# A two-layer encoder trunk in split float32: the second SwiGLU's first column pair as Strassen products, the root mean square from a table, and smaller moves

## The chip, the cores and the metric

The kernel runs on one core of one Trainium2 chip. The metric is the device time in microseconds, as the median of the runs. A profiled execution is a run of its own, with a time of its own.

## What is computed

Two layers over 512 tokens of width 1024, each a half-step SwiGLU, a mixer (gated convolution and latent attention with a rotation of the positions), a second half-step SwiGLU and a gated projection of a per-layer input; then a last norm. The functions that the change touches:

```python
def rmsnorm(x, g):
    xf = x.astype(jnp.float32)
    y = xf * lax.rsqrt(jnp.mean(xf * xf, axis=-1, keepdims=True) + EPS)
    return (y * g.astype(jnp.float32)).astype(x.dtype)

def swiglu(x, w_gu, w_down):
    g, u = jnp.split(x @ w_gu, 2, axis=-1)
    return (jax.nn.silu(g) * u) @ w_down

def apply_rope(x, cos, sin):
    ...
    return jnp.concatenate([x1 * cos - x2 * sin, x2 * cos + x1 * sin], axis=-1).astype(x.dtype)

def reference(...):
    h = x
    for i in range(DEPTH):
        h = h + 0.5 * swiglu(rmsnorm(h, ffn1_norm[i]), ffn1_w_gu[i], ffn1_w_down[i])
        u = rmsnorm(h, mix_norm[i])
        ...
        h = h + merged @ w_o[i]
        h = h + 0.5 * swiglu(rmsnorm(h, ffn2_norm[i]), ffn2_w_gu[i], ffn2_w_down[i])
        gate = jax.nn.sigmoid(rmsnorm(h, ple_norm[i]) @ w_ple_gate[i])
        h = h + gate * (p[i] @ w_ple_proj[i])
    return rmsnorm(h, final_norm)
```

## The kernel before

**Split numbers.** All matrix work is float32 by three products: each operand is split into a rounded part (ACT's cast, names that end in h) and the rest (DVE's subtraction, names that end in l), and PE multiplies hh, lh and hl (`mm3`, L209 to L211). Weights stream from HBM in packed blocks of 128x1024: SP loads one into `st`, ACT makes `wh` (L67), DVE makes `wl` (L68). Four such pairs are in use at a time, and ten raw blocks.

**Strassen products.** Most wide products are done in 2x2 blocks with seven products instead of eight. `Quad.part` gives the weight sums (L138 to L149, each a DVE step of 128x1024, ahead of another wh and wl), `Halved.row` the token sums of row j (L379 to L386: x and y scaled on ACT, four DVE steps of 128x256 into t and u, then the splits th, tl, uh, ul). `Sevens.step(n, j)` issues product j of column pair n into three PSUM banks (tiles b0nb, b0nc, b0na); products 1, 5 and 6 are copied out by ACT (L434). Product 1 uses the split x of rows 0 to 3, product 5 the left half of t, 6 and 4 the halves of u, 7 the right half of t, 2 and 3 the split x of rows 4 to 7.

**One SwiGLU (`ffn`).** Its name is a0 or a1 (first SwiGLU of layer 0 or 1), b0 or b1 (second). `normed` splits the eight blocks of h as they become final and sums their squares; `rms` turns the sum into r = 1/rms, by which the products are scaled afterwards. The first columns are computed whole, without Strassen, over the eight blocks x0 to x7 (4 gate and up pairs in a0, 2 elsewhere); PE has this work while DVE forms the token sums. In a1 rows 0 and 1 of the token sums stand ahead, among the last blocks of h; in b0 and b1 all four come after h. Then come the Strassen products, each pair's last ones alternating with the next pair's first, and the down projection.

**What sets the order.** There is no planner: each engine runs its instructions in one queue, in the order that results from the program's order and the scheduler's priorities. A step that waits holds up all behind it on its engine.

**rms.** A matmul with ones sums the squares over the partitions (ps); DVE scales (L282), ACT takes the root (L283, after a table load), DVE takes the reciprocal (L284) and a Newton step (L285 to L287).

**The end.** The last block's sigmoid, product and sum (L870 to L873), squares on ACT (L887), a PE sum (`fss`), DVE, ACT and DVE for 1/rms (L919 to L926), then the scaled output tiles `fo` (L932, L934) and their DMAs.

## Time and profile before

| | us |
|---|---|
| median of 3 runs | 2299.07 (2299.01 to 2299.6) |
| profiled execution, its own time | 2300.29 |
| its span | 2298.4 |
| PE busy | 2278.3 (99%) |
| DVE busy | 1866.4 (81%) |
| ACT busy | 1123.8 (49%) |
| mean granted clock of PE | 0.997 |

The span runs from the first instruction to the last write; the profiled execution's own time is 1.89 us longer. PE's busy share counts pipelined matmuls, so it doesn't show small holes; waits do. Time lies in the timeline by its start from the span's start: a0 begins at 0, b0's first matmul is at 747.42, a1 begins near 1148, the last output is issued at 2294.18.

### The profile page before, as it was taken

To read this page: it belongs to the slowest core of one execution; us is meant where nothing else is said; L and a number is where in the kernel's file an instruction comes from. 1 tells how busy PE (TensorE), PEld (TensorE's weight loads), DVE (VectorE), ACT (ScalarE), POOL (GpSimd) and SP (SyncE) were. 2 spreads that over 40 slices of the span, in tenths; PEclk is the share of its full clock that TensorE was granted. 3 is DMA by queue.
4 is the path that set the end of the run, shared out by engine and by line. 5 is a ranking of instruction groups with operands and counts; after the bars stand their busy time and mean duration, and the time that the engine had idled before them with its cause. 6 is when DMAs were issued, how large, how long until landed. Compare 5 with 4: busy or idle time off the path is not lost.

```text
span 2298.4 us, 34687 instructions
## 1 busy us (share of the span) xinstructions
PE 2278.3 (99%) x14168; PEld 2061.6 (90%) x14168; DVE 1866.4 (81%) x2577; ACT 1123.8 (49%) x1682; POOL 36.8 (2%) x42
## 2 busy tenths in 40 slices
...
GB/s 193 110 92 103 100 142 92 55 120 120 55 61 87 65 120 101 102 111 129 82 74 111 102 101 115 118 89 74 108 104 56 74 73 101 103 100 101 110 83 38
DMA packets 63087, 222.76 MB, mean 97 GB/s; under 512 B 7248, under 2 KB 7248, under 8 KB 62928
## 3 DMA queue, kind: packets, MB, share of 16 engines
...
q10 hardware_dynamic: 720, 0.84, 0.1%
q14 instruction: 48, 0.39, 0.1%
...
## 4 chain that ended last, share of the span: by engine, by line
PE 93%; DVE 5%; ACT 1%; issue 1%; DMA 0%; ACTq 0%
PE a0pd L209 2%; PE a1pd L209 2%; PE b0pd L209 2%; PE b1pd L209 2%; PE b1pd L210 2%; PE b0pd L210 2%; PE a1pd L210 2%; PE a0pd L210 2%; PE a0pd L211 2%; PE a1pd L211 2%; PE b0pd L211 2%; PE b1pd L211 2%; DVE wl L68 1%; PE e1gp L209 1%; PE e1gp L211 1%; PE e1gp L210 1%
## 5 line engine op out<-in xcount | busy, mean ns | idle before, releaser
L67 ACT CAST wh<-st 128x1024 fp32r<-128x1024 f32 (+1 forms) x456 | 475.2, 1043 | 559.9 <-issue 59.5
L68 DVE TENSOR_TENSOR wl<-st,wh 128x1024 fp32r<-128x1024 f32 (+1 forms) x456 | 552.2, 1212 | 149.5 <-ACT wh L67 148.9
L67 ACT CAST wh<-s 128x1024 fp32r<-128x1024 f32 x94 | 98.8, 1052 | 124.0 <-PE a0pd L210 8.5
L68 DVE TENSOR_TENSOR wl<-s,wh 128x1024 fp32r<-128x1024 f32 x94 | 114.5, 1218 | 16.4 <-ACT wh L67 16.3
L146 DVE TENSOR_TENSOR st<-st,s 128x1024 f32<-128x1024 f32 x47 | 57.5, 1222 | 1.1
L143 DVE TENSOR_TENSOR s<-s,st 128x1024 f32<-128x1024 f32 x47 | 57.3, 1220 | 0.1
L138 DVE TENSOR_TENSOR s<-st,st 128x1024 f32<-128x1024 f32 x47 | 57.3, 1219 | 0.1
L149 DVE TENSOR_TENSOR st<-st,st 128x1024 f32<-128x1024 f32 x47 | 57.3, 1219 | 0.1
L499 DVE SCALAR_TENSOR_TENSOR h<-b0pd,h 128x512 f32<-128x512 f32 x40 | 27.5, 688 | 8.9 <-PE b0pd L211 8.8
L499 DVE SCALAR_TENSOR_TENSOR h<-b1pd,h 128x512 f32<-128x512 f32 x40 | 27.6, 689 | 8.8 <-PE b1pd L211 8.8
L499 DVE SCALAR_TENSOR_TENSOR h<-a1pd,h 128x512 f32<-128x512 f32 x40 | 27.5, 688 | 7.4 <-PE a1pd L211 7.3
L499 DVE SCALAR_TENSOR_TENSOR h<-a0pd,h 128x512 f32<-128x512 f32 x40 | 27.5, 687 | 6.8 <-PE a0pd L211 6.8
L103 POOL MEMSET wh<- 128x256 f32 x4 | 1.1, 312 | 1201.3 <-DVE wl L68 1201.3
L786 DVE TENSOR_TENSOR m0g<-m0mop,m0g 128x512 f32<-128x512 f32 x8 | 5.5, 691 | 6.5 <-PE m0mop L211 6.5
L283 ACT ACT_TABLE_LOAD x8 | 10.3, 1283 | 0.1
L786 DVE TENSOR_TENSOR m1g<-m1mop,m1g 128x512 f32<-128x512 f32 x8 | 5.5, 691 | 5.9 <-PE m1mop L211 5.8
L791 DVE TENSOR_TENSOR h<-m1wop,h 128x512 f32<-128x512 f32 x8 | 5.5, 691 | 4.1 <-PE m1wop L211 4.1
L791 DVE TENSOR_TENSOR h<-m0wop,h 128x512 f32<-128x512 f32 x8 | 5.5, 691 | 4.1 <-PE m0wop L211 4.1
L887 ACT ACTIVATE fsq<-h 128x256 f32<-128x256 f32 (+1 forms) x11 | 5.2, 471 | 6.0 <-DVE h L873 6.0
L871 ACT ACT_TABLE_LOAD x3 | 3.8, 1283 | 8.3 <-DVE e_g L870 8.3
L637 DVE TENSOR_TENSOR m1g<-m1cop,m1g 128x512 f32<-128x512 f32 x8 | 5.5, 690 | 2.5 <-PE m1cop L211 2.5
L637 DVE TENSOR_TENSOR m0g<-m0cop,m0g 128x512 f32<-128x512 f32 x8 | 5.5, 689 | 2.5 <-PE m0cop L211 2.5
...
## 6 DMA issues: line engine op xcount, KB each, us to landing
...
```

What stands on the lines that cost most here:

```text
L67: self.nc.scalar.copy(hi[:, w], src[:, w])
L68: self.nc.vector.tensor_tensor(lo[:, w], src[:, w], hi[:, w].bitcast(F32), ALU.subtract)
L138: tt(self.s, self.a21, self.a22, ALU.add)
L143: tt(self.s, self.s, self.a11, ALU.subtract)
L146: tt(self.a12, self.a12, self.s, ALU.subtract)
L149: tt(self.a11, self.a11, self.a21, ALU.subtract)
L209: nc.tensor.matmul(ps, wh, vh, start=first, stop=False)
L210: nc.tensor.matmul(ps, wh, vl, start=False, stop=False)
L211: nc.tensor.matmul(ps, wl, vh, start=False, stop=last)
L499: nc.vector.scalar_tensor_tensor(h[m], ps, 0.5, h[m], ALU.mult, ALU.add)
L637: nc.vector.tensor_tensor(gates[m], ps, gates[m], ALU.mult)
L786: nc.vector.tensor_tensor(t, mla_ps[m], t, ALU.mult)
```

## The change

It has five parts.

1. In b0 and b1 no column is computed whole any more. The first pair becomes Strassen products too, whose products 1 and 5 stand at once behind w_o's last block on PE; the token sums of rows 0 to 2 and the left half of row 3 stand among w_o's last blocks on DVE. The a SwiGLUs keep their whole columns, and in a1 rows 0 and 1 move ahead by some places.
2. `rms` takes 1/sqrt from an ACT table; Square and the scaling move from DVE to ACT too, and DVE keeps the last two steps.
3. `rope` copies the four swapped blocks of 32 rows on ACT and multiplies by sin once, at full height, on DVE.
4. At the end, the table for 1/sqrt is loaded beside the last product and sum; the last squares and gains are on DVE, and the three partial sums add up in PSUM.
5. At the start the gains' DMA (`cols`) goes from ACT's queue to GpSimd's, the first wh is cast on DVE, and the first row of a0 is issued part by part.

```diff
@@ Stream.split
-            self.nc.scalar.copy(hi[:, w], src[:, w])
+            if i == c == 0:
+                self.nc.vector.tensor_copy(hi[:, w], src[:, w])
+            else:
+                self.nc.scalar.copy(hi[:, w], src[:, w])
@@ projs (called with part_by_part for a0 only)
+            if k == 0 and part_by_part:
+                for ps, (wh, _) in zip(pss, ws):
+                    nc.tensor.matmul(ps, wh, vh, start=True, stop=False)
...
@@ setup
-    nc.scalar.dma_start(out=cols, in_=gains)
+    nc.gpsimd.dma_start(out=cols, in_=gains)
...
@@ rms
-        nc.vector.tensor_scalar(ms, ps, 1.0 / n, EPS, ALU.mult, ALU.add)
-        nc.scalar.activation(t, ms, AF.Sqrt)
-        nc.vector.reciprocal(r, t)
-        nc.vector.tensor_tensor(t, r, r, ALU.mult)
+        nc.scalar.activation(r, ps, AF.Abs_reciprocal_sqrt, scale=1.0 / n, bias=eps_t)
+        nc.scalar.activation(t, r, AF.Square)
+        nc.scalar.activation(ms, ps, AF.Identity, scale=1.0 / n, bias=eps_t)
         nc.vector.scalar_tensor_tensor(t, t, -0.5 * scale, ms, ALU.mult, ALU.mult)
         nc.vector.scalar_tensor_tensor(r, t, 1.5 * scale, r, ALU.add, ALU.mult)
@@ Halved: row(j) is now own(j), then other(j)
+        def own(self, j, xs, parts=False):
...
+            nc.scalar.mul(x, h[j], gain(self.nm, self.l, j))
+            nc.vector.tensor_tensor(t[:, left], x[:, right], x[:, left], ALU.subtract)
+            th, tl = G(f"{self.name}t{j}h", F32R), G(f"{self.name}t{j}l", F32R)
+            if parts:
+                split_to(th[:, left], tl[:, left], t[:, left])
...
+        def other(self, j, xs):
...
+            nc.scalar.mul(y, h[k], gain(self.nm, self.l, k))
+            nc.vector.tensor_tensor(t[:, right], y[:, right], x[:, right], ALU.subtract)
...
@@ ffn
-    def ffn(l, nm, name, first=False, beside=None, early=False):
+    def ffn(l, nm, name, first=False, beside=None, early=2):
-        n_early = KD // 2 - 2 if early else 0
...
-        n_whole = 4 if first else 2
+        n_whole = 4 if first else 0 if early > 2 else 2
+        def early_rows(k, xs):
+            j = k - KD // 2
+            if 0 <= j < early:
+                ys.row(j, xs)
+            if n_whole == 0 and k == KD - 2:
+                ys.own(KD // 2 - 1, xs, True)
+                step(0, 1)
+                step(0, 5)
+        xs, acc = normed(nm, l, name, early_rows)
+        if n_whole == 0:
+            ys.other(KD // 2 - 1, xs)
+            r = rms(acc, D, name)
+            order = (2, 6, 3)
...
@@ rope
-        nc.vector.tensor_tensor(t1, src, cos, ALU.mult)
         for a in range(0, P, 64):
             for o, i in ((a, a + 32), (a + 32, a)):
-                nc.vector.tensor_tensor(t2[o:o + 32, :], src[i:i + 32, :], sin[i:i + 32, :], ALU.mult)
+                nc.scalar.copy(t2[o:o + 32, :], src[i:i + 32, :])
+        nc.vector.tensor_tensor(t1, src, cos, ALU.mult)
+        nc.vector.tensor_tensor(t2, t2, sin, ALU.mult)
@@ the last block: ple_add, Final.add, Final.finish
+        if end:
+            nc.scalar.activation(warm, s[:, 0:1], AF.Abs_reciprocal_sqrt)
...
+                nc.vector.tensor_tensor(sq, hk, hk, ALU.mult)
+                nc.vector.tensor_scalar(self.hg[k][:, toks], hk, gain("final", 0, k), None, ALU.mult)
...
+            nc.scalar.activation(r, ss[:, :nt], AF.Abs_reciprocal_sqrt, scale=1.0 / D, bias=eps_t)
             nc.vector.tensor_scalar(ms, ss[:, :nt], 1.0 / D, EPS, ALU.mult, ALU.add)
-            for c in (4, 8):
-                nc.vector.scalar_tensor_tensor(ms, ss[:, c:c + nt], 1.0 / D, ms, ALU.mult, ALU.add)
-            nc.scalar.activation(rt, ms, AF.Sqrt)
-            nc.vector.reciprocal(r, rt)
@@ calls
-        ffn(l, "ffn1", f"a{l}", l == 0, rotary if l == 0 else None, l > 0)
+        ffn(l, "ffn1", f"a{l}", l == 0, rotary if l == 0 else None, 2 if l else 0)
-        ffn(l, "ffn2", f"b{l}")
+        ffn(l, "ffn2", f"b{l}", early=3)
```

PE loses 96 matmuls of 128x512 in each of b0 and b1 and gains 168 of 128x256 (14281 instructions in all instead of 14137).

**b0 on DVE** (b1 is the same), from the sum that ends w_o's block 6 (h6). Before:

```order
L791 TENSOR_TENSOR h6_95<-m0wop6_7154,h6_95 128x512
L205 SCALAR_TENSOR_TENSOR b0x6l_7260<-h6_95,cols_87,b0x6h_7259 128x512
L270 TENSOR_TENSOR b0acc_7222<-b0acc_7222,b0sq_7263 128x512
L68 TENSOR_TENSOR wl170_7356<-st131_7353,wh170_7355 128x1024
L791 TENSOR_TENSOR h7_96<-m0wop7_7186,h7_96 128x512
L68 TENSOR_TENSOR wl171_7386<-st132_7383,wh171_7385 128x1024
L205 SCALAR_TENSOR_TENSOR b0x7l_7267<-h7_96,cols_87,b0x7h_7266 128x512
L270 TENSOR_TENSOR b0acc_7222<-b0acc_7222,b0sq_7270 128x512
L138 TENSOR_TENSOR s_7753<-st138_7681,st139_7683 128x1024
L202 TENSOR_TENSOR b0al_7274<-b0acc_7222,b0ah_7273 128x512
L383 TENSOR_TENSOR b0t0_7415<-b0x0_7413 128x256
```

Now, from the same row:

```order
L828 TENSOR_TENSOR h6_95<-m0wop6_7155,h6_95 128x512
L392 TENSOR_TENSOR b0t1_7279<-b0x1_7278 128x256
L146 TENSOR_TENSOR s_7369<-s_7369,st129_7329 128x1024
L408 TENSOR_TENSOR b0t1_7279<-b0y1_7284,b0x1_7278 128x256
L152 TENSOR_TENSOR st129_7329<-st129_7329,st130_7331 128x1024
L409 TENSOR_TENSOR b0u1_7285<-b0t1_7279,b0x1_7278 128x256
L71 TENSOR_TENSOR wl170_7437<-st132_7335,wh170_7436 128x1024
L410 TENSOR_TENSOR b0u1_7285<-b0y1_7284,b0u1_7285 128x256
L828 TENSOR_TENSOR h7_96<-m0wop7_7187,h7_96 128x512
L205 TENSOR_TENSOR b0t1l_7283<-b0t1_7279,b0t1h_7282 128x512
L71 TENSOR_TENSOR wl171_7471<-s_7369,wh171_7470 128x1024
```

and on from there:

```order
L205 TENSOR_TENSOR b0u1l_7293<-b0u1_7285,b0u1h_7292 128x512
L149 TENSOR_TENSOR st132_7335<-st132_7335,s_7369 128x1024
L208 SCALAR_TENSOR_TENSOR b0x6l_7297<-h6_95,cols_78,b0x6h_7296 128x512
L282 TENSOR_TENSOR b0acc_7223<-b0acc_7223,b0sq_7300 128x512
L392 TENSOR_TENSOR b0t2_7304<-b0x2_7303 128x256
L71 TENSOR_TENSOR wl172_7502<-st132_7335,wh172_7501 128x1024
L408 TENSOR_TENSOR b0t2_7304<-b0y2_7309,b0x2_7303 128x256
L409 TENSOR_TENSOR b0u2_7310<-b0t2_7304,b0x2_7303 128x256
L410 TENSOR_TENSOR b0u2_7310<-b0y2_7309,b0u2_7310 128x256
L205 TENSOR_TENSOR b0t2l_7308<-b0t2_7304,b0t2h_7307 128x512
L205 TENSOR_TENSOR b0u2l_7318<-b0u2_7310,b0u2h_7317 128x512
```

Before, three steps stood between h6 and h7, and the token sums (b0t0, ...) came after h7 and the sum of squares. Now row 1's sums, two weight sums (L146, L152) and a wl stand between h6 and h7, the splits of row 1, a third weight sum (L149), x6l and row 2's sums behind h7, and the rest t2l of row 2's t comes 20 steps after h6; row 3's follows it (u2l, then two steps of 128x256 for t3).

**b0 on PE**, at the end of w_o. Before:

```order
L211 MATMUL m0wop7_7186<-m0mg7h_6958,wl167_7202 128x512
L209 MATMUL b0pg0_7277<-b0x0h_7218,wh168_7281 128x512
L210 MATMUL b0pg0_7277<-b0x0l_7219,wh168_7281 128x512
L211 MATMUL b0pg0_7277<-b0x0h_7218,wl168_7282 128x512
L209 MATMUL b0pu0_7278<-b0x0h_7218,wh168_7281 128x512
L210 MATMUL b0pu0_7278<-b0x0l_7219,wh168_7281 128x512
L211 MATMUL b0pu0_7278<-b0x0h_7218,wl168_7282 128x512
```

Now the 24 matmuls of product 1 (x0 to x3) follow w_o and then those of product 5, six to each of t0, t1, t2, t3; here where t1 meets t2:

```order
L442 MATMUL b00c_7368<-b0t1h_7282,wh169_7371 128x256
L442 MATMUL b00c_7368<-b0t1l_7283,wh169_7371 128x256
L442 MATMUL b00c_7368<-b0t1h_7282,wl169_7372 128x256
L442 MATMUL b00c_7368<-b0t2h_7307,wh169_7371 128x256
L442 MATMUL b00c_7368<-b0t2l_7308,wh169_7371 128x256
L442 MATMUL b00c_7368<-b0t2h_7307,wl169_7372 128x256
```

Before, PE had 98 matmuls of 128x512 here ahead of the first Strassen product; now product 5's t2 is the 37th matmul of 128x256 after w_o.

**a0 on DVE**, where 1/rms is made. Before:

```order
L282 TENSOR_SCALAR a0ms_318<-a0ps_313 128x512
L68 TENSOR_TENSOR wl7_422<-st7_419,wh7_421 128x1024
L284 RECIPROCAL a0r_316<-a0t_317 128x512
L383 TENSOR_TENSOR a0t3_505<-a0x3_503 128x256
L285 TENSOR_TENSOR a0t_317<-a0r_316 128x512
L384 TENSOR_TENSOR a0t3_505<-a0y3_504,a0x3_503 128x256
L286 SCALAR_TENSOR_TENSOR a0t_317<-a0t_317,a0ms_318 128x512
L385 TENSOR_TENSOR a0u3_506<-a0t3_505,a0x3_503 128x256
L287 SCALAR_TENSOR_TENSOR a0r_316<-a0t_317,a0r_316 128x512
L386 TENSOR_TENSOR a0u3_506<-a0y3_504,a0u3_506 128x256
L202 TENSOR_TENSOR a0t3l_514<-a0t3_505,a0t3h_513 128x512
```

Now:

```order
L71 TENSOR_TENSOR wl7_421<-st7_418,wh7_420 128x1024
L409 TENSOR_TENSOR a0u1_473<-a0t1_467,a0x1_466 128x256
L410 TENSOR_TENSOR a0u1_473<-a0y1_472,a0u1_473 128x256
L298 SCALAR_TENSOR_TENSOR a0t_317<-a0t_317,a0ms_318 128x512
L205 TENSOR_TENSOR a0t1l_471<-a0t1_467,a0t1h_470 128x512
L299 SCALAR_TENSOR_TENSOR a0r_316<-a0t_317,a0r_316 128x512
L205 TENSOR_TENSOR a0u1l_481<-a0u1_473,a0u1h_480 128x512
L392 TENSOR_TENSOR a0t2_485<-a0x2_484 128x256
L408 TENSOR_TENSOR a0t2_485<-a0y2_490,a0x2_484 128x256
L409 TENSOR_TENSOR a0u2_491<-a0t2_485,a0x2_484 128x256
L410 TENSOR_TENSOR a0u2_491<-a0y2_490,a0u2_491 128x256
```

L282, the reciprocal L284 and L285 are gone from DVE's queue, and the two steps that are left stand beside row 1 instead of row 3.

**a1 on DVE**, ahead of x6l. Before:

```order
L270 TENSOR_TENSOR a1acc_11128<-a1acc_11128,a1sq_11180 128x512
L873 TENSOR_TENSOR h7_96<-h7_96,e0g7_11119 128x512
L383 TENSOR_TENSOR a1t1_11185<-a1x1_11183 128x256
L384 TENSOR_TENSOR a1t1_11185<-a1y1_11184,a1x1_11183 128x256
L138 TENSOR_TENSOR s_11659<-st214_11587,st215_11589 128x1024
L385 TENSOR_TENSOR a1u1_11186<-a1t1_11185,a1x1_11183 128x256
L386 TENSOR_TENSOR a1u1_11186<-a1y1_11184,a1u1_11186 128x256
L68 TENSOR_TENSOR wl278_11401<-st209_11391,wh278_11400 128x1024
L202 TENSOR_TENSOR a1t1l_11194<-a1t1_11185,a1t1h_11193 128x512
L202 TENSOR_TENSOR a1u1l_11198<-a1u1_11186,a1u1h_11197 128x512
L205 SCALAR_TENSOR_TENSOR a1x6l_11202<-h6_95,cols_87,a1x6h_11201 128x512
```

Now:

```order
L392 TENSOR_TENSOR a1t1_11285<-a1x1_11284 128x256
L71 TENSOR_TENSOR wl279_11398<-st207_11395,wh279_11397 128x1024
L408 TENSOR_TENSOR a1t1_11285<-a1y1_11290,a1x1_11284 128x256
L409 TENSOR_TENSOR a1u1_11291<-a1t1_11285,a1x1_11284 128x256
L410 TENSOR_TENSOR a1u1_11291<-a1y1_11290,a1u1_11291 128x256
L908 TENSOR_TENSOR e0g7_11220<-e0gp7_11182,e0r_10943 128x512
L205 TENSOR_TENSOR a1t1l_11289<-a1t1_11285,a1t1h_11288 128x512
L205 TENSOR_TENSOR a1u1l_11299<-a1u1_11291,a1u1h_11298 128x512
L914 TENSOR_TENSOR e0g7_11220<-e0pp7_11183,e0g7_11220 128x512
L208 SCALAR_TENSOR_TENSOR a1x6l_11303<-h6_95,cols_78,a1x6h_11302 128x512
L915 TENSOR_TENSOR h7_96<-h7_96,e0g7_11220 128x512
```

Row 1's sums and their splits stand ahead of the last block's product and h7 (L914, L915), and x6l four steps behind the first step of that last block (L908); before, it stood nine places behind h7's own row.

## Rows read from the trace of the kernel before

**Rows 1.** The page, parts 1 and 4: engines, and the chain that ended last.

```profile
PE 2278.3 (99%) x14168; PEld 2061.6 (90%) x14168; DVE 1866.4 (81%) x2577; ACT 1123.8 (49%) x1682; POOL 36.8 (2%) x42
...
PE 93%; DVE 5%; ACT 1%; issue 1%; DMA 0%; ACTq 0%
```

**Rows 2.** Timeline, PE, b0: start us, duration, instruction, count, [idle before <-releaser].

```profile
747.42 0.39 PE L209 MATMUL b0pg<-b0x0h,wh 128*128 128x512 f32 x1
...
769.67 0.28 PE L415 MATMUL b01b<-b0x0h,wh 128*128 128x256 f32 x1
...
783.94 0.28 PE L415 MATMUL b02b<-b0x3h,wl 128*128 128x256 f32 x1
```

**Rows 3.** Timeline, PE, the two waits in a0.

```profile
63.29 0.38 PE L415 MATMUL a03b<-a0x0h,wh 128*128 128x256 f32 x1 [0.44 <-ACT wh L67]
...
67.88 0.58 PE L415 MATMUL a02c<-a0x4h,wh 128*128 128x256 f32 x1 [4.21 <-ACT a02c L434]
```

**Rows 4.** Windows: stretch, length, busy us (count) by engine, PEclk, DMA share, GB/s.

```profile
66.50:67.00 0.50, 0.00 (x0) 0.00 (x0) 0.50 (x2) 0.06 (x1) 0.00 (x0) 0.81 0.01 0
67.00:73.50 6.50, 5.62 (x26) 5.62 (x27) 4.30 (x6) 2.66 (x5) 0.00 (x0) 0.50 0.50 149
```

**Rows 5.** Timeline, DVE, 1/rms of a0.

```profile
35.82 0.68 DVE L282 TENSOR_SCALAR a0ms<-a0ps 128x512 f32<-128x512 f32 x1
...
38.73 3.35 DVE L284 RECIPROCAL a0r<-a0t 128x512 f32<-128x512 f32 x1 [1.09 <-ACT a0t L283]
```

**Rows 6.** Timeline, ACT, a0: a silu ahead of the copy that PE awaits.

```profile
66.94 0.42 ACT L482 ACTIVATE a02c<-a02c 128x256 f32<-128x256 f32 x1 [1.37 <-DVE a02c L481]
```

**Rows 7.** Timeline, DVE, b0: last two blocks of h.

```profile
742.18 0.69 DVE L791 TENSOR_TENSOR h<-m0wop,h 128x512 f32<-128x512 f32 x1 [0.59 <-PE m0wop L211]
...
747.62 0.69 DVE L791 TENSOR_TENSOR h<-m0wop,h 128x512 f32<-128x512 f32 x1 [0.59 <-PE m0wop L211]
```

**Rows 8.** Timeline, DVE, a1: steps back to back.

```profile
1152.53 0.42 DVE L384 TENSOR_TENSOR a1t<-a1y,a1x 128x256 f32<-128x256 f32 x1
1152.86 1.22 DVE L138 TENSOR_TENSOR s<-st,st 128x1024 f32<-128x1024 f32 x1
1154.00 0.42 DVE L385 TENSOR_TENSOR a1u<-a1t,a1x 128x256 f32<-128x256 f32 x1
1154.45 0.43 DVE L386 TENSOR_TENSOR a1u<-a1y,a1u 128x256 f32<-128x256 f32 x1
...
1156.53 0.69 DVE L202 TENSOR_TENSOR a1u1l<-a1u,a1u1h 128x512 fp32r<-128x512 f32 x1
1157.13 0.75 DVE L205 SCALAR_TENSOR_TENSOR a1x6l<-h,cols,a1x6h 128x512 fp32r<-128x512 f32 x1
```

**Rows 9.** Timeline, PE: waits in b0 and a1.

```profile
784.80 0.39 PE L415 MATMUL b01c<-b0x4h,wh 128*128 128x256 f32 x1 [0.58 <-ACT b01c L434]
...
1157.94 0.50 PE L210 MATMUL a1pg<-a1x6l,wh 128*128 128x512 f32 x1 [0.84 <-DVE a1x6l L205]
...
1190.42 0.39 PE L415 MATMUL a11b<-a1t0h,wl 128*128 128x256 f32 x1 [0.48 <-DVE wl L68]
```

**Rows 10.** Timeline, ACT and DVE, the end.

```profile
2290.48 1.28 ACT L922 ACT_TABLE_LOAD   x1
...
2291.77 0.20 ACT L922 ACTIVATE fr<-fr 128x2 f32<-128x2 f32 x1
...
2292.01 0.17 DVE L923 RECIPROCAL fr<-fr 128x2 f32<-128x2 f32 x1 [0.70 <-ACT fr L922]
...
2292.86 0.72 ACT L932 ACTIVATE fo<-fu,fr 128x512 f32<-128x512 f32 x1 [0.88 <-DVE fr L926]
```

**Rows 11.** Timeline, ACT and PE, the start.

```profile
4.00 0.72 ACT L204 ACTIVATE a0x0h<-h,cols 128x512 fp32r<-128x512 f32 x1 [0.86 <-DMA cols<-in_gains]
...
6.15 0.50 PE L209 MATMUL a0pg<-a0x0h,wh 128*128 128x512 f32 x1 [1.03 <-ACT wh L67]
```

**Rows 12.** One tile's instructions (rotation, one head pair): duration ns min/median/max, first and last start.

```profile
L543 DVE TENSOR_TENSOR m0h0qrt<-m0h0qr,sinT x4: 681/686/695, 567.1 to 569.2; 32x512 f32<-32x512 f32 x4
```

More of the change, by code (lines that the diff above doesn't have):

```diff
@@ L236, in trunk_kernel @@
     nc.vector.memset(hpi, math.pi / 2)
-    cols = cp.tile([P, gains.shape[1]], F32, tag="cols", name="cols")
-    nc.scalar.dma_start(out=cols, in_=gains)
     col_at = {}
@@ L307, in trunk_kernel @@
     for i in range(8):
-        nc.tensor.matmul(idle[:, :P], ident, ident, start=True, stop=True)
+        nc.tensor.matmul(idle[:, :P], ones.bitcast(F32), ones.bitcast(F32), start=True, stop=True)
     pt_w = [max(2, NT - j) * P for j in range(NT)]
@@ L366, in __init__ @@
             self.ys = {p_: [] for p_ in range(1, 8)}
+            self.half = {}
         def row(self, j, xs):
+            self.own(j, xs)
+            self.other(j, xs)
+        def own(self, j, xs, parts=False):
             H = S // 2
             left, right = slice(0, H), slice(H, S)
-            name, k = self.name, j + KD // 2
-            def halves_of(hi_lo, *ps_):
-                for at, p_ in zip((left, right), ps_):
-                    if p_:
-                        self.ys[p_].append(tuple(t[:, at] for t in hi_lo))
@@ new lines, in own @@
+            if parts:
+                split_to(th[:, left], tl[:, left], t[:, left])
+            self.ys[1].append(tuple(v[:, left] for v in xs[j]))
+            self.ys[5].append((th[:, left], tl[:, left]))
+            self.half[j] = x, t, th, tl, parts
+        def other(self, j, xs):
+            H = S // 2
+            left, right = slice(0, H), slice(H, S)
+            k = j + KD // 2
+            x, t, th, tl, parts = self.half.pop(j)
+            y, u = G(f"{self.name}y{j}"), G(f"{self.name}u{j}")
+            nc.scalar.mul(y, h[k], gain(self.nm, self.l, k))
+            nc.vector.tensor_tensor(t[:, right], y[:, right], x[:, right], ALU.subtract)
+            nc.vector.tensor_tensor(u[:, left], t[:, right], x[:, left], ALU.add)
+            nc.vector.tensor_tensor(u[:, right], y[:, left], u[:, left], ALU.subtract)
+            at = right if parts else slice(0, S)
+            split_to(th[:, at], tl[:, at], t[:, at])
+            uh, ul = split(u, f"{self.name}u{j}")
+            for p_, v, at in ((2, xs[k], left), (3, xs[k], right), (7, (th, tl), right), (6, (uh, ul), left), (4, (uh, ul), right)):
+                self.ys[p_].append(tuple(w[:, at] for w in v))
```

105 lines of the change are left out of this document (49 added, 56 removed).

## Prediction

> **What bounds the kernel now.** I read the page first. PE is busy 99% of the span and the chain that ended last is PE's to 93%; DVE has 81% [rows 1]. So time goes only where PE has less to do, where it waits, or where its clock is low, and an engine beside it matters only where PE runs into it. PE's pace then comes from its timeline. From 747.42 to 769.67 it issues 98 matmuls of 128x512, from there to 783.94 another 119 of 128x256, without a hole [rows 2]: 22.25 / 98 = 0.227 us and 14.27 / 119 = 0.120 us from start to start. The duration in a row (0.39, 0.28) is longer, since matmuls overlap. Last I went through PE's waits stage by stage. The large ones are in a0: 0.44 us for a wh and 4.21 us for ACT's copy of product 5 [rows 3]. The windows show that the granted clock falls behind that hole (0.81 in 66.5 to 67) and is 0.50, its level of 1.2 GHz, through 73.5 [rows 4]. Smaller waits stand in b0 and a1 [rows 9] and at both ends [rows 10, 11].
>
> The profiled execution took 2300.29 us, 1.22 above the median of the runs shown. I sum the differences against it and apply them to the median, 2299.07. About 0.2% (4.6 us) is what a measurement of this kernel can tell from no change.
>
> **1/rms from the table, in a0.** DVE loses the scaling, the reciprocal with its wait, and one product. The rows give 0.60 to the next start for the first and the last (0.68 less the overlap of 0.08 that neighbouring steps show [rows 8]), 1.09 of wait and 3.27 for the reciprocal (3.35 less that overlap) [rows 5]: 0.60 + 1.09 + 3.27 + 0.60 = 5.56 us. From there to the silu at 66.94, which itself waits for DVE [rows 6], DVE is busy almost without a pause, so the 5.56 us pass on to that silu, and to the copy behind it. PE gets the copy at 67.88 now; it would be there at 67.88 - 5.56 = 62.3. PE has nothing before that product from about 63.7 on, and about 0.4 less once a03b's first matmul no longer stands ahead of it. So the copy comes some 1 us before PE asks. That takes away both waits (4.65) and the low clock: from 67.88 to 73.5 PE pays 5.62 us for what takes 5.62 x 0.120 / 0.216 = 3.12 at the high clock, where 0.216 is 5.62 / 26 [rows 4]. The gain is 4.65 + 2.50 = 7.15, taken as **-7.2**. At least 3.5 should be left if something else on DVE or ACT is late (below); no more than 8 with the refill of PE's pipeline after a hole.
>
> **The same in the other uses** of full width frees 4.5 to 5.6 us of DVE each. PE waits for none of these r today except through DVE's backlog, so this is worth 0 by itself.
>
> **The second SwiGLU's first pair (b0, b1).** PE loses 96 x 0.227 = 21.8 us of whole columns and gains 168 x 0.120 = 20.2: -1.6 in each layer. The Trainium skill, "TensorE: Matmul & The Clock Gate", section "Wait — 56ns, not 53.3ns?", gives 215.7 ns for N = 512 warm, by its formula about 109.2 for 256; that would make it 20.7 - 18.3 = -2.4 in each layer, 1.5 less in the sum. The rows measure this kernel's own matmuls, so I stay with them.
>
> But these 21.8 us of whole columns are what PE does today while DVE forms the token sums, and the cover is gone. Products 1 and 5 follow w_o at once. PE reaches t2 after 36 matmuls: 747.42 + 36 x 0.120 = 751.74. DVE can't have t2l by then. Its queue from h6, which cannot start before PE ends that block at 742.18 [rows 7], holds ahead of t2l six steps of 1024 at 1.14, five of 512 at 0.60, x6l at 0.67 and eight of 256 at 0.33 (two of them behind their own operand, 0.45), from the steps back to back [rows 8]: 6.84 + 3.00 + 0.67 + 2.64 + 0.24 = 13.4, and 0.68 for t2l itself: 756.3 at the earliest. PE waits at least 4.5 us; with some hand-overs to ACT I take **4.9**. Then t3l: behind t2l stand u2l (0.60), the left half of t3 (0.33), ACT's cast of it (0.42, as a half-width step [rows 6]) and its rest (0.42), 1.8 in all, and PE has six matmuls for it, 0.72 at the high clock and 1.28 at the low: **0.6** more (0.5 to 1.2). A hole of 4.2 us has dropped the clock in a0, so I take it to fall here as well, at about the price seen there, **2.3** (0 to 2.5). Last, DVE is behind by then with the weights of products 7 and the second pair: **0.5** (0 to 1.0). That is 8.3. Against it stand the -1.6 and today's own wait in b0, 0.58 [rows 9], which gets other surroundings and is counted as gone: 8.3 - 1.6 - 0.6 = **+6.1** in each layer, **+12.2** in both. The bounds are 4.5 + 0.5 - 2.2 = +2.8 and 5.2 + 1.2 + 2.5 + 1.0 - 2.2 = +7.7 each.
>
> **a1.** x6l is 0.84 late and a wl 0.48 [rows 9]. Row 1's sums now stand ahead of the last block's steps, x6l comes four steps behind the first of these, and the reciprocal's 3.3 us no longer delay the wl. Both waits should go: **-1.3** (0 to -1.7).
>
> **The end.** Today the chain runs over a table load at 2290.48 (1.28), root 2291.77, reciprocal 2292.01 to the first output tile at 2292.86 [rows 10]. With the load beside the last product, the 1/sqrt can start when the sum is there, about when the load starts now plus 0.3; the root's wait of 1.0 and the reciprocal's 0.20 go: **-1.2** (0 to -1.5). The skill's "ScalarE: Activation LUTs", section "What ACT_TABLE_LOAD costs", adds a drain of 1380 ns to the load, 2.66 us for a switch; here the next ACT step starts 1.29 us after the load [rows 10], so the trace shows no drain. With one, the new load would end about 0.7 us too late, and the gain would be 0.5.
>
> **The start.** The first matmul is at 6.15, behind wh, whose raw block was issued behind the gains on ACT's queue; x0h waits for the gains until 4.00 [rows 11]. The weights go out some 0.45 earlier, and wh no longer stands behind x0h on ACT: **-0.5**. How fast GpSimd's queue delivers the gains, no row shows: up to +1.0 if x0h gets late.
>
> **Rotation.** Four steps of 32 rows leave DVE for ACT and one of full height comes: 4 x 0.686 [rows 12] less 0.6, 2.1 us of DVE less for each head pair. ACT has 49% [rows 1], PE waits there for other things: 0 (-0.5 to +1.0 for each of eight pairs).
>
> **Sum:** -7.2 + 12.2 - 1.3 - 1.2 - 0.5 = +2.0, so **2301.0 us**: less than a measurement can tell.
>
> **Rivals.**
>
> *Faster: the second SwiGLUs cost only the bound.* The clock holds, since the two holes in b0 are shorter or lie apart, and DVE catches up at once: +2.8 in each layer, 5.6 in both, and -4.6 in the sum: 2294.5; with the refill in a0 (0.8) 2293.7. For it: the clock's fall is seen once, and only just behind such a hole. Against it: 4.9 us is longer than a0's 4.2. It decides if PEclk stays at 1.00 in both.
>
> *Slower: a0's copy stays late.* The copy stands on ACT behind a silu and a cast, and the margin is about 1 us. ACT gets three steps of 512 for each 1/rms and the new token sums' casts stand elsewhere; if the copy is 4 us later than I say, PE idles 3 us, and half of the clock's price comes back: 3 + 1.3 of the 7.2 lost, 2305.3. With b0 at its upper bound as well, 2308.5. For it: PE runs through a0 close behind DVE on every product. Against it: DVE's 5.6 us are a sum of rows. It decides from an idle of about 2.5 us ahead of product 3 in a0.
>
> *Slower: the rotation's copies hold up the mixers.* ACT makes wh and the splits of the next heads there; 1.0 us of PE for each of eight pairs gives 2309. ACT's share speaks against it.
>
> **How the numbers follow.** Forecast 0.53, the faster rival 0.22, the late copy 0.19, the rotation 0.06. The forecast's own range is about 2297 to 2305. The range that leaves out 2 in 10 runs from **2294.0** to **2307.5**. Faster by over 0.2% (under 2294.5) is half of the first rival and the forecast's lower tail (0.08): **0.20**. Slower (over 2303.7) is most of the two slower rivals (0.18) and the forecast's upper tail (0.10): **0.28**. The same: **0.52**.
>
> **What would show it.** In a0, PE's product 3 of pair 2 starts without a wait for ACT's copy, and PEclk stays at 1.00 there. In b0 and b1, PE waits 4 to 5 us at t2 with t2l or t2h as what released it, then at t3, with PEclk at 0.50 for some 5 us; DVE has no pause from h6 to t3l. x6l in a1 releases no wait. No table load stands between the last sum of squares and the first `fo` any more. The prediction is wrong if PE passes t2 without a wait of 4 us, or if product 3 in a0 waits over 2.

## The result and the profile after

The changed kernel takes 2305.99 us (median of 7 runs, 2304.4 to 2308.34), the kernel before 2299.19 beside it (7 runs, 2298.9 to 2299.6): ratio 1.0031, 95% interval 1.0019 to 1.0043. That is 0.3% slower. The forecast was 2301.0, 5.0 us (0.2%) less; the range (2294.0 to 2307.5) holds the time, but what had the largest chance ("the same", 0.52) did not happen, and "slower" (0.28) did. The runs of the changed kernel also lie 4 us apart, those of before 0.7.

The profiled execution took 2307.06 us, its span is 2305.2. Its page, parts 1 and 4, beside [rows 1]:

```profile
PE 2281.8 (99%) x14312; PEld 2070.9 (90%) x14312; DVE 1816.6 (79%) x2534; ACT 1170.0 (51%) x1762; POOL 34.7 (2%) x43
...
PE 95%; DVE 3%; ACT 1%; issue 0%; DMA 0%; ACTq 0%; POOLq 0%
```

PE is as busy as before and the chain is still PE's, now to 95%. Shares don't show what happened; the start times of the same matmuls in both timelines do. "Here" is what a stage adds or takes away. An idle time in brackets in the timeline is shorter than what PE loses from start to start, since a matmul's row is longer than its pace: the 3.75 below is 4.03 from start to start (746.93 to 750.96), 3.91 more than the pace of 0.12.

| PE reaches | before | after | behind by | here |
|---|---|---|---|---|
| first matmul (a0pg) | 6.15 | 6.71 | +0.56 | +0.56 |
| product 6 of pair 2 in a0 | 59.32 | 61.14 | +1.82 | +1.26 |
| first matmul of mixer 0 | 360.94 | 354.55 | -6.39 | -8.21 |
| last matmul of its w_o | 747.19 | 742.51 | -4.68 | +1.71 |
| first down projection in b0 | 811.38 | 813.22 | +1.84 | +6.52 |
| first down projection in a1 | 1213.07 | 1212.55 | -0.52 | -2.36 |
| last matmul of w_o in mixer 1 | 1881.21 | 1882.38 | +1.17 | +1.69 |
| first down projection in b1 | 1945.39 | 1953.18 | +7.79 | +6.62 |
| last two matmuls (ft, the last transposes), start | 2290.58 | 2298.38 | +7.80 | 0 |
| end of the span | 2298.4 | 2305.2 | +6.8 | -1.0 |

The waits of PE by line, longest first, show the places (engine, line, who waited for whom, total us, times, longest):

```profile
PE b10c L442 <- ACT b1t2h L204: 3.8, 1, 3.8
PE b00c L442 <- ACT b0t2h L204: 3.7, 1, 3.7
PE a0pg L230 <- ACT a0x0h L207: 1.9, 1, 1.9
...
PE b01a L442 <- ACT wh L70: 0.8, 1, 0.8
```

The 4.2 us in a0 [rows 3] are gone, 3.7 and 3.8 in b0 and b1 have come, and the first real matmul waits 1.9 for x0h. **b0** in the timeline, PE first, then DVE:

```profile
750.96 0.38 PE L442 MATMUL b00c<-b0t2h,wh 128*128 128x256 f32 x1 [3.75 <-ACT b0t2h L204]
...
751.84 0.39 PE L442 MATMUL b00c<-b0t2l,wh 128*128 128x256 f32 x1 [0.49 <-DVE b0t2l L205]
...
753.40 0.58 PE L442 MATMUL b00c<-b0t3h,wh 128*128 128x256 f32 x1 [0.35 <-ACT b0t3h L204]
```

```profile
737.69 0.68 DVE L828 TENSOR_TENSOR h<-m0wop,h 128x512 f32<-128x512 f32 x1
...
743.04 0.68 DVE L828 TENSOR_TENSOR h<-m0wop,h 128x512 f32<-128x512 f32 x1
...
749.85 0.41 DVE L408 TENSOR_TENSOR b0t<-b0y,b0x 128x256 f32<-128x256 f32 x1
...
751.09 0.69 DVE L205 TENSOR_TENSOR b0t2l<-b0t,b0t2h 128x512 fp32r<-128x512 f32 x1
...
753.38 0.43 DVE L205 TENSOR_TENSOR b0t3l<-b0t,b0t3h 128x256 fp32r<-128x256 f32 x1 [0.47 <-ACT b0t3h L204]
```

From h6 (743.04 is h7, 737.69 h6) to t3l DVE has next to no pause until the last row's 0.47, and from h6 to t2l it takes 13.40 us (737.69 to 751.09); the right half of t2 comes at 749.85, ACT casts it at 750.29 and PE, whose last matmul of t1 starts near 746.9, waits until 750.96, then for t2l and for t3. The windows behind the hole (stretch, length, busy us and count by engine, PEclk) read:

```profile
748.00:752.00 4.00, 0.55 (x2) 0.35 (x3) 3.85 (x8) 2.38 (x5) 0.00 (x0) 1.00 0.64 177
752.00:759.00 7.00, 6.65 (x30) 6.19 (x31) 3.83 (x6) 4.25 (x8) 0.00 (x0) 0.51 0.12 49
759.00:765.00 6.00, 6.00 (x50) 5.92 (x50) 2.82 (x6) 5.19 (x9) 0.00 (x0) 1.00 0.00 0
```

The granted clock is at its 1.2 GHz level for seven microseconds behind the hole, as it was in a0 before [rows 4]. **The start** [rows 11] and the first five microseconds behind it:

```profile
5.94 0.72 ACT L207 ACTIVATE a0x0h<-h,cols 128x512 fp32r<-128x512 f32 x1 [3.27 <-DMA cols<-in_gains]
...
6.71 0.50 PE L230 MATMUL a0pg<-a0x0h,wh 128*128 128x512 f32 x1 [1.93 <-ACT a0x0h L207]
```

```profile
7.00:12.00 5.00, 5.00 (x16) 3.92 (x16) 4.70 (x8) 5.00 (x10) 0.00 (x0) 0.66 1.04 397
```

x0h waits for the gains until 5.94, and PE then issues 16 matmuls in 5 us where the kernel before has 22. **The mixer**'s loss lies at its first head pair. ACT copies four blocks of 32 rows behind a gate's step, DVE waits 2.9 us for them, and PE's weight loads then wait for the splits of q and k:

```profile
560.72 2.35 ACT L578 COPY m0h0qrt<-m0h0qr 32x512 f32<-32x512 f32 x4
...
563.09 0.69 DVE L579 TENSOR_TENSOR m0h0qrt<-m0h0qr,cosT 128x512 f32<-128x512 f32 x1 [2.88 <-ACT m0h0qrt L578]
```

```profile
PEld m0s01p L758 <- issue: 0.6, 2, 0.3
PEld m0s00p L761 <- DVE m0h0qr L726: 0.5, 1, 0.5
PEld m0s01p L758 <- ACT m0h0qn1h L204: 0.4, 1, 0.4
PEld m0s01p L760 <- DVE m0h0qn1l L205: 0.2, 1, 0.2
PEld m0s00p L760 <- DVE m0h0qn0l L205: 0.2, 1, 0.2
```

Between the first score of that pair (m0s00p) and the first matmul of the next pair's q (m0h1qr) PE takes 8.15 us (566.84 to 574.99) where the kernel before takes 6.45 (573.18 to 579.63), 1.70 more; from there on the mixer takes no longer than before, 1.7 in all at the end of w_o.

**a0**: ACT's copy is there before PE asks; product 3 of pair 2 starts without an idle time, against 4.21 of [rows 3]:

```profile
62.23 0.58 ACT L461 COPY a02c<-a02c 128x512 f32<-128x512 f32 x1
...
64.02 0.28 PE L442 MATMUL a02c<-a0x4h,wh 128*128 128x256 f32 x1
```

**The end** [rows 10]: the table load stands beside the last product, and `fo` starts 0.94 behind the start of the 1/sqrt:

```profile
2296.49 1.28 ACT L913 ACT_TABLE_LOAD   x1
...
2298.56 0.26 ACT L965 ACTIVATE fr<-fss,eps_t 128x2 f32<-128x2 f32 x1 [0.57 <-PE fss L946]
...
2299.50 0.72 ACT L975 ACTIVATE fo<-fu,fr 128x512 f32<-128x512 f32 x1 [0.68 <-DVE fr L969]
```

### The profile page after: what moved, and what is told of

Read it like the earlier page. It is cut to its first block, busy times and chain, and to the rows that moved or that the text cites. A ratio compares the mean times of both kernels' runs of the same rounds, so it can differ in the third digit from the quotient of the medians.

```text
span 2305.2 us, 35035 instructions
## 1 busy us (share of the span) xinstructions
PE 2281.8 (99%) x14312; PEld 2070.9 (90%) x14312; DVE 1816.6 (79%) x2534; ACT 1170.0 (51%) x1762; POOL 34.7 (2%) x43
## 3 DMA queue, kind: packets, MB, share of 16 engines
q8 instruction: 112, 1.84, 0.3%
## 4 chain that ended last, share of the span: by engine, by line
PE 95%; DVE 3%; ACT 1%; issue 0%; DMA 0%; ACTq 0%; POOLq 0%
PE b0pd L212 2%; PE a1pd L212 2%; PE a0pd L212 2%; PE b1pd L212 2%; PE a0pd L213 2%; PE a1pd L213 2%; PE b0pd L213 2%; PE b1pd L213 2%; PE b1pd L214 2%; PE a0pd L214 2%; PE a1pd L214 2%; PE b0pd L214 2%; DVE wl L71 1%; PE e1gp L212 1%; PE e1gp L214 1%; PE e1gp L213 1%
## 5 line engine op out<-in xcount | busy, mean ns | idle before, releaser
L71 DVE TENSOR_TENSOR wl<-s,wh 128x1024 fp32r<-128x1024 f32 x98 | 119.4, 1218 | 16.0 <-ACT wh L70 16.0
L149 DVE TENSOR_TENSOR st<-st,s 128x1024 f32<-128x1024 f32 x49 | 59.9, 1222 | 1.1
L146 DVE TENSOR_TENSOR s<-s,st 128x1024 f32<-128x1024 f32 x49 | 59.8, 1220 | 0.2
L152 DVE TENSOR_TENSOR st<-st,st 128x1024 f32<-128x1024 f32 x49 | 59.7, 1218 | 0.1
```

The costliest lines, as they stand in the source:

```text
L71: self.nc.vector.tensor_tensor(lo[:, w], src[:, w], hi[:, w].bitcast(F32), ALU.subtract)
L146: tt(self.s, self.s, self.a11, ALU.subtract)
L149: tt(self.a12, self.a12, self.s, ALU.subtract)
L152: tt(self.a11, self.a11, self.a21, ALU.subtract)
```

## The experiments

All stages in one table, worked out as above from the timeline of each run's one profiled execution: what each stage adds to the kernel before, in us. The medians and intervals are against the kernel before on the same chip.

| kernel | median | ratio (95%) | to product 6 in a0 | rest of a0 | m0 | b0 | a1 | m1 | b1 |
|---|---|---|---|---|---|---|---|---|---|
| changed | 2305.99 | 1.0031 (1.0019, 1.0043) | +1.82 | -8.21 | +1.71 | +6.52 | -2.36 | +1.69 | +6.62 |
| e1_b_whole | 2289.34 | 0.9959 (0.9945, 0.9974) | -0.02 | -8.18 | +1.68 | -1.40 | -2.35 | +1.78 | -1.38 |
| e2_rope_dve | 2302.82 | 1.0014 (1.0004, 1.0023) | +2.74 | -8.22 | +0.09 | +5.88 | -2.37 | +0.07 | +5.49 |
| e3_cols_act | 2305.66 | 1.0031 (1.0020, 1.0041) | +2.71 | -8.23 | +1.71 | +6.62 | -2.35 | +1.70 | +6.64 |
| e4_fill | 2302.77 | 1.0015 (1.0006, 1.0025) | -0.11 | -8.22 | +1.69 | +4.65 | -2.35 | +1.67 | +4.67 |
| e5_no_sums | 2301.54 | 1.0014 (1.0004, 1.0023) | +1.72 | -8.19 | +1.69 | +3.93 | -2.35 | +1.70 | +3.72 |
| e6_rms_dve | 2320.32 | 1.0095 (1.0080, 1.0110) | +1.78 | -7.11 | +1.74 | +11.16 | +0.18 | +1.70 | +11.03 |
| e7_best | 2290.44 | 0.9963 (0.9950, 0.9976) | +1.36 | -5.94 | +0.09 | -1.39 | -2.35 | +0.09 | -1.39 |
| e8_best_sp | 2285.71 | 0.9943 (0.9923, 0.9963) | -0.41 | -8.22 | +0.12 | -1.39 | -2.37 | +0.13 | -1.39 |
| e9_table_only | 2292.41 | 0.9967 (0.9955, 0.9980) | +0.89 | -3.76 | +0.08 | -1.40 | -2.35 | +0.09 | -1.38 |
| e10_best10 | 2285.74 | 0.9942 (0.9930, 0.9955) | -0.39 | -8.23 | +0.10 | -1.39 | -2.35 | +0.13 | -1.39 |
| e11_start_before | 2308.72 | 1.0043 (1.0028, 1.0059) | +1.40 | -6.49 | +1.70 | +5.49 | -2.36 | +1.74 | +6.02 |

**e1_b_whole** undoes the second SwiGLU's part.

```diff
-        ffn(l, "ffn2", f"b{l}", early=3)
+        ffn(l, "ffn2", f"b{l}", early=0)
```

> The changed kernel with b0 and b1 as before (first pair computed whole, all token sums after h). Theory: the second SwiGLUs' boundaries cost 6.5 us each in the changed kernel, because DVE's queue from h6 to t2l is longer than PE's 36 matmuls; both go, so 2306 - 13 = 2293, and the clock stays at 1.00 behind w_o. Rival (the loss comes from elsewhere, the low clock at other places or DVE's new load): no more than 5 us come back, 2301 or above.

16.7 us come back, more than the 13: b0 and b1 are now 1.4 faster than in the kernel before each, since the table (e9) takes their old waits [rows 9] too. So the all-Strassen boundary costs 6.5 + 1.4 = 7.9 us in each layer, 15.8 in both. The remaining 0.9 is within what the start does from one execution to the next: this one's happened to run at the high clock, with 24 matmuls in the stretch that had 16 above:

```profile
7.00:12.00 5.00, 5.00 (x24) 4.12 (x23) 4.70 (x9) 5.00 (x10) 0.00 (x0) 1.00 1.05 399
```

**e2_rope_dve** undoes the rotation's part, in `rope` (and the sign in its table).

```diff
-                nc.scalar.copy(t2[o:o + 32, :], src[i:i + 32, :])
+                nc.vector.tensor_tensor(t2[o:o + 32, :], src[i:i + 32, :], sin[i:i + 32, :], ALU.mult)
```

> The changed kernel with the rotation as before (four steps of 32 rows on DVE, no copies on ACT). Theory: ACT's four copies, behind the last gate, hold DVE up 2.9 us ahead of the first head pair of each mixer and cost PE about 1.7 us in each, hidden in the other pairs: 2306 - 3.5 = 2302.5, and the first pair's scores start without holes. Rival (copies cost nothing, the holes come from the weights): 2306. Rival (each of eight pairs pays): 2298.

As the theory had it: the mixers' +1.7 each are gone, and they were lost at the first pair alone; the other pairs never paid.

**e3_cols_act** moves the gains' DMA alone.

```diff
-    nc.gpsimd.dma_start(out=cols, in_=gains)
...
+    nc.scalar.dma_start(out=cols, in_=gains)
     warm = cp.tile([P, 1], F32, tag="warm", name="warm")
```

> The changed kernel with the gains' DMA on ACT's queue, behind the first weights. Theory: on GpSimd's queue the gains take 4.7 us and make x0h late, the first matmul comes at 6.7 and the clock falls to half until about 11.3; with the DMA on ACT's queue the first matmul comes at about 5.4 and the clock stays high: 0.56 + 0.75 + 1.75 less, 2303. Rival (the low clock at the start comes from the shorter run of idle matmuls, not from the wait): 1.3 less, 2304.7, with PEclk at 0.5 still.

The theory fell. Next to nothing came back (0.3 in the median, less than the spread of the runs), and the gains are nearly as late from ACT's queue, issued at 1.16 behind the weights:

```profile
5.70 0.72 ACT L207 ACTIVATE a0x0h<-h,cols 128x512 fp32r<-128x512 f32 x1 [2.56 <-DMA cols<-in_gains]
```

So it is not GpSimd's queue that is slow: gains that are issued behind a large transfer land after 4.5 to 4.7 us from either queue; first in ACT's queue, at 0.71, they were there by 4.00 [rows 11]. And the low clock is here too, though the clock column doesn't say so: 13 matmuls in 5 us, 0.43 from start to start up to 12.2, then 0.23.

```profile
7.00:12.00 5.00, 5.00 (x13) 3.87 (x12) 4.70 (x9) 5.00 (x10) 0.00 (x0) 1.00 1.02 355
```

**e4_fill** puts 40 matmuls into the hole, ahead of product 5 of the first pair in b0 and b1.

```diff
         def product(self, ps, d, j, fill=0):
             hi, lo = d["w"].part(j)
+            for _ in range(fill):
+                nc.tensor.matmul(ps[:, 0, :], hi[:, :P], self.ys[j][0][0], start=True, stop=True, skip_group_check=True)
```

> The changed kernel with 40 matmuls of 128x256 more in b0 and b1, ahead of product 5 of the first pair, into the bank that it then overwrites: they fill the hole ahead of t2 (40 x 0.12 = 4.8 us) and change no result. Theory: the hole itself can't be shortened by them, but the clock stays at 1.00 behind it, which gives back about 2.3 us in each layer: 2301.5. Rival (behind the hole ACT and DVE set the pace, not the clock): within 1 us of 2306, with PE waiting for t3, x7 or weights instead.

b0 and b1 cost 4.65 instead of 6.5 and the clock stays high behind the hole:

```profile
752.00:754.00 2.00, 2.00 (x17) 2.00 (x18) 0.18 (x1) 1.26 (x2) 0.00 (x0) 1.00 0.00 0
754.00:756.00 2.00, 2.00 (x19) 2.00 (x19) 2.00 (x3) 1.42 (x3) 0.00 (x0) 1.00 0.00 0
```

PE reaches t3's first matmul as far behind w_o as without the 40 (10.9 us in b0), so they delay nothing, and 1.9 us in each layer is the clock's price in the profile of the changed kernel, 3.8 in both (the median shows 3.2); the rest is the hole's. That price is not fixed: in e2 and e11, where b0 and b1 have the same code and t2h the same wait (3.77 or 3.78), the clock falls while PE still waits (in the changed kernel's profile over 1 us after the wait) and these stages cost 5.5 to 6.0, so 0.8 to 1.4 for the clock.

**e5_no_sums** takes weight sums out of DVE's queue; its products use raw weight quarters, so its output isn't the reference's.

```diff
+        if self.plain and j in (5, 6, 3):
+            return W.split({5: self.a21, 6: self.a22, 3: self.a12}[j])
```

> The changed kernel, but the first pair of b0 and b1 takes products 5, 6 and 3 with raw weight quarters: the weight sums are left out (so the output isn't the reference's). In DVE's queue two steps of 128x1024 fewer stand between h6 and t2l, and a third stands ahead of h6. Theory (DVE's queue decides when t2 comes): t2 comes 2.3 to 3.4 us earlier, the hole on PE shrinks from 5 to about 2, the clock stays at 1.00 and its price (about 2) goes too: 4.5 to 5.3 less in each layer, 2306 - 10 = 2296. Rival (ACT's casts or h7 decide): 2304 or above, with the same hole.

Between the two: 2.6 and 2.9 us less in the layers, not 4.5 to 5.3. t2 comes 1.9 earlier against t1 (waits of 1.88 and 0.49, and then t3), so DVE's queue does decide; the rest of the 2.6 and 2.9 is no more than the clock's price varies by (e4). What is left is not DVE's queue alone: DVE waits 0.47 for a wh ahead of t1l, and the t2h cast follows t2 on ACT. The hole left is still enough to drop the clock:

```profile
748.99 0.38 PE L444 MATMUL b00c<-b0t2h,wh 128*128 128x256 f32 x1 [1.88 <-ACT b0t2h L206]
...
749.86 0.38 PE L444 MATMUL b00c<-b0t2l,wh 128*128 128x256 f32 x1 [0.49 <-DVE b0t2l L207]
```

```profile
752.00:754.00 2.00, 2.00 (x10) 2.00 (x11) 0.00 (x0) 0.89 (x1) 0.00 (x0) 0.50 0.00 0
```

**e6_rms_dve** undoes the table in `rms`.

```diff
-        nc.scalar.activation(r, ps, AF.Abs_reciprocal_sqrt, scale=1.0 / n, bias=eps_t)
-        nc.scalar.activation(t, r, AF.Square)
-        nc.scalar.activation(ms, ps, AF.Identity, scale=1.0 / n, bias=eps_t)
+        nc.vector.tensor_scalar(ms, ps, 1.0 / n, EPS, ALU.mult, ALU.add)
+        nc.scalar.activation(t, ms, AF.Sqrt)
+        nc.vector.reciprocal(r, t)
+        nc.vector.tensor_tensor(t, r, r, ALU.mult)
```

> The changed kernel with 1/rms as before (scaling, root, reciprocal and product, on DVE but for the root). Theory: it is the reciprocal that made a0's copy late, so a0's waits and its low clock come back, 7 to 9 us, a1's two waits too, about 1 to 2; b0 and b1 have 4.9 us more on DVE behind x7, of which 0 to 1 shows: 2306 + 9.5 = 2315. Rival (a0 gained from the order of its products and the table matters little): 2306 to 2309.

The total is 5 us worse than expected, and not where I had it: a0 keeps 7.1 of its 8.2 us without the table, while b0 and b1 get 4.6 and 4.4 worse (in b0 PE waits 1.02 for a wh, 1.09 for a wl and 1.27 for a copy by ACT where the changed kernel has one wait of 0.78). a1's gain is gone (+0.18), so that is the table's. In a0 PE has other matmuls in the hole's place, eleven of a03b's and one of the down projection's ahead of product 3:

```profile
65.20 0.50 PE L212 MATMUL a0pd<-a0a0h,wh 128*128 128x512 f32 x1 [0.82 <-ACT wh L70]
...
66.61 0.28 PE L443 MATMUL a02c<-a0x4h,wh 128*128 128x256 f32 x1
```

**e7_best** keeps the table and the end, and has b0, b1, the rotation and the start as before: the edits of e1 and e2, and for the start

```diff
-            if i == c == 0:
-                self.nc.vector.tensor_copy(hi[:, w], src[:, w])
...
-        pss = projs(sum(cs[:n], []), xs, sum(names[:n], []), first)
+        pss = projs(sum(cs[:n], []), xs, sum(names[:n], []))
-    nc.gpsimd.dma_start(out=cols, in_=gains)
+    nc.scalar.dma_start(out=cols, in_=gains)
-        nc.tensor.matmul(idle[:, :P], ones.bitcast(F32), ones.bitcast(F32), start=True, stop=True)
+        nc.tensor.matmul(idle[:, :P], ident, ident, start=True, stop=True)
```

> The table for 1/rms and the new end kept; b0 and b1, the rotation and the start as before. Theory: the parts are independent, so from the 2289.3 of the kernel with only b0 and b1 undone the mixers give back 2 x 1.7 and the start 0.3 (first matmul at 6.15): 2285.5, and the runs lie within 1 us, since the clock at the start no longer falls in some of them. Rival (the start of before is no better): 2286 with runs 2 us apart.

5 us slower than expected. The stages that I thought independent aren't: with the old start, a03b's first matmul stands ahead of product 3 again, ACT's copy comes only at 65.24, and a wait is left in a0 (-5.94 instead of -8.2). It is the copy that costs: in e8 below three matmuls of a03b stand ahead of product 3, the copy is there at 60.02, and PE doesn't wait. The low clock at the start came all the same (+1.36 though the first matmul is at 5.65):

```profile
65.86 0.39 PE L439 MATMUL a02c<-a0x4h,wh 128*128 128x256 f32 x1 [2.03 <-ACT a02c L458]
```

**e8_best_sp** has rows 0 and 1 early in b0 and b1 (beside the whole columns), the rotation of before, and the changed start with two edits.

```diff
-    nc.gpsimd.dma_start(out=cols, in_=gains)
+    nc.sync.dma_start(out=cols, in_=gains)
-    for i in range(8):
+    for i in range(12):
-        ffn(l, "ffn2", f"b{l}", early=3)
+        ffn(l, "ffn2", f"b{l}", early=2)
```

> As the last, but rows 0 and 1 of the token sums early in b0 and b1 too, the changed kernel's start with the gains' DMA first on SyncE's queue, and 12 idle matmuls instead of 8. Theory: what made x0h late is that the gains are issued behind weights and x, so first in a queue they land by about 4.2, the first matmul comes at about 5.4, and there is no long hole: 0.7 less than the last, 2284.8. b0 and b1 without a wait in either. Rival (weights and x are then as much later): as the last or slower, 2285.5 to 2286.5.

The fastest: 13 us under the kernel before. x0h no longer waits for the gains but for x, the idle matmuls reach to the first real one, and the list of PE's waits has nothing over 0.9 behind the start:

```profile
4.85 0.72 ACT L207 ACTIVATE a0x0h<-h,cols 128x512 fp32r<-128x512 f32 x1 [2.19 <-DMA h<-in_x]
...
6.15 0.47 PE L230 MATMUL a0pg<-a0x0h,wh 128*128 128x512 f32 x1
```

```profile
PE idle L320 <- DVE hpi L250: 1.0, 1, 1.0
PE m0s10p L757 <- DVE m0h1qn1l L205: 0.9, 1, 0.9
PE m1s10p L757 <- DVE m1h1qn1l L205: 0.9, 1, 0.9
PE fss L945 <- DVE fsq L926: 0.8, 1, 0.8
```

**e9_table_only** is the kernel before with the table alone, e6's diff the other way round.

> The kernel before with one part of the change alone: 1/rms from the table. Theory: DVE's freed time shortens a0's hole from 4.2 to 2 us and keeps the clock high there (-5.9, as in the kernel with start, rotation and second SwiGLUs as before), and takes away today's small waits in b0 and b1 (-1.4 each) and in a1 (-2.3): 2299.0 - 11 = 2288. Rival (a0's hole is set by the order of PE's products and not by DVE): a0 gains under 2, 2293 or above.

Between theory and rival. b0 and b1 gain just what they gain in e1, a1 what it gains in the changed kernel, so those parts are the table's. a0 gains 3.8, not 5.9: the hole shrinks only to 2.73 and the clock falls still. Of DVE's 5.6 freed microseconds 2.9 turn into new waits for ACT (3.6 in all, of which 0.7 was there before), and this execution's start is 0.9 late, so the copy comes 1.8 earlier. PE's row, DVE's waits from 30 to 67, and the window behind the hole:

```profile
66.10 0.39 PE L414 MATMUL a02c<-a0x4h,wh 128*128 128x256 f32 x1 [2.73 <-ACT a02c L433]
```

```profile
DVE a0t L382 <- ACT a0x L378: 1.4, 1, 1.4
DVE wl L68 <- ACT wh L67: 0.8, 3, 0.3
DVE a0a1l L202 <- ACT a0a1h L201: 0.7, 1, 0.7
DVE a0t L285 <- ACT a0ms L284: 0.7, 1, 0.7
```

```profile
66.00:74.00 8.00, 7.90 (x53) 7.90 (x54) 6.09 (x10) 4.24 (x7) 0.00 (x0) 0.79 0.44 133
```

**e10_best10** is e8 with fewer idle matmuls.

```diff
-    for i in range(12):
+    for i in range(10):
```

> The fastest version so far with 10 idle matmuls at the start instead of 12. Theory: with 12 the idle matmuls themselves last until the first real one at 6.15, while its operands are there at 5.6: first matmul at 5.65 and 2285.2, runs within 0.5 us. Rival (the shorter run of idle matmuls lets the clock fall at the start in some runs): 2287, runs 2 us apart.

No gain; four of the five runs lie within 0.4 us and one is 2.2 above. The first matmul comes at 5.47, 0.68 earlier, and PE is no further at product 6 (-0.39 against -0.41): from 7 to 12 it is busy for 4.71 of 5 us, with 0.28 of wait for the split of x1 (a0x1l) as the longest.

**e11_start_before** undoes the start's part alone, with e7's diff of the start.

> The changed kernel with the start as before (gains first on ACT's queue, first wh cast on ACT, first row of a0 in the old order, idle matmuls behind the identity). Theory: the first matmul comes 1.1 earlier (5.65), but with the old start a03b's first matmul stands ahead of product 3 of pair 2 again and a hole of 2 us is left in a0: about +1 on balance, 2306 to 2308. Rival (the changed start costs 2.3 us by its low clock, and a0 gains from the table alone): 2303.5.

Slightly worse than the changed kernel, near the theory, though the intervals of the two overlap: the first matmul at 5.76 doesn't help (+1.40 by product 6, again at the low clock), and a0 loses 1.7 of its gain. The copy for product 3 comes at 64.74, behind the silu's step on DVE at 63.70, ahead of which DVE has seven weight steps of 128x1024 from 52.5 on; in the changed kernel it has three of them from 52.2 on and is at that step by 59.74.

## Why the prediction was right or wrong

**Right: the second SwiGLU's hole.** The sum of DVE's steps said 13.4 us from h6 to t2l, and they took 13.40; so t2l can't be there within 4.5 us, most likely 4.9, then 0.6 for t3 and a low clock. Measured from start to start: 3.9 for t2h, 0.8 for t2l, 0.6 for t3; e4 puts the clock at 1.9 (2.3 in the prediction), and one wh later PE waits 0.78 (0.5). The idle times alone, 3.75 and 0.49, are 4.2 and only just over the 4 that the prediction named as its sign. The stage came to +6.5 and +6.6 where the sum said +6.1, and that is nearer than its terms: without the table's 1.4 it would have been 7.9, where the sum has 8.3 - 1.6 = 6.7. The -1.6 of PE's own work holds: from the last matmul of w_o to the first down projection the rows of e1 have 99 matmuls of 128x512 and 336 of 128x256, which at 0.227 and 0.120 take all of its 62.79 us; the changed kernel has 3 and 504, 61.2 of its 70.7 us, so 9.5 are holes and low clock where the prediction had 8.3. e5 shows that DVE's queue is the cause, with less effect than its steps alone say.

**Right in size, wrong in reason: a0.** The gain is 8.2 where I took 7.2, and the copy came at 62.23 with PE asking at 64.02. The missing 1.0 is in the kernel before: from start to start the two waits cost 5.1 and not 4.65, and PE loses 0.5 more in small gaps at the start of product 6 (59.32 to 60.17). But the step "the 5.56 us pass on to that silu" failed: in e9, where nothing else changes, the silu's copy is only 1.8 earlier, because ACT's new three steps delay the x that DVE needs next. What closed the hole in the changed kernel is the table together with another order of the work: the table alone gives 3.8 (e9), the table with the rest of the change but the old start, and so the copy at 65.24 and 64.74, 5.9 and 6.5 (e7, e11), the rest of the change without the table 7.1, with other matmuls in the hole's place (e6). That the sum came near was luck. Part of that order comes with the start's lines (e7, e11); which of the other changed lines set it was not tried.

**Wrong: the start**, term -0.5, bound +1.0. It cost +1.8 in the profiled execution: 0.56 for the late gains, which the bound had, and 1.3 for the low clock, which nothing in the sum had. That 1.3 can't be put down to the change: with the same start code e1 and e4 have the high clock and are level with the kernel before by product 6 (-0.02, -0.11), e2 has, by PE's pace, the low one (+2.74); and with the start of before e7, e9 and e11 have the low clock too (+0.89 to +1.40, their first matmul at 5.61 to 5.76 instead of 6.15). So the gain of 0.5 didn't come, since x0h waits for the gains in place of wh, and the rest is by execution. Why the clock is low in one and not in another stays open. In e8 and e10, whose idle matmuls end later (the last starts at 6.10 and 5.25, not 4.41), it was high in the one profile of each. The start and the price of the clock in b0 and b1, which vary from profile to profile, are likely why the runs of the changed kernel lie 4 us apart; only one execution of it has a trace, so this is not shown.

**Wrong: the rotation**, term 0. I looked at ACT's mean share and at each of eight pairs alike. The first pair of each mixer has no work of another pair beside it: 1.7 us each, 3.4 in all (e2), which the rival had per pair but not by place.

**Sizes: a1** gained 2.4, not 1.3. Its two idle times [rows 9] are 1.3, but from start to start, with the slower matmuls beside them, PE loses 1.3 about x6l and 0.8 about the wl, and 0.2 more where the sum of squares (a1ps) begins; none of this is left in the changed kernel. It is the table's and not that of the earlier rows of the token sums, as the prediction had it for x6l: e9 has the gain without them, and e6, which has them, still waits 0.74 for x6l. **The end** gave 1.0 (1.2). The Trainium skill ("ScalarE: Activation LUTs", section "What ACT_TABLE_LOAD costs") counts a drain of about 1380 ns with the load at a switch of tables. It isn't seen here either: ACT's next step is at 2297.79, 1.30 behind the load's start.

The sum of what was off is +2.3 (start), +3.4 (rotation), -1.0 (a0), -1.1 (a1), +0.9 (b0 and b1), +0.2 (end): +4.7 of the 5.0 us between forecast and result. Errors of +6.8 and -2.1 stand against each other in it; had a0 and a1 given no more than their terms, the time would have been about 2308, outside the range. That the range holds is in part luck.
